# Seven quarter products in place of eight for the latent keys and six gate tiles

## The chip, the cores and the metric

The kernel runs on one core of a Trainium2 chip. Its time is the device time of one execution in microseconds (us); three runs gave 587.22 to 587.62, median 587.51. A core has five engines with a queue of instructions each, worked off in order: TensorE (PE) multiplies matrices into PSUM, VectorE (DVE) and ScalarE (ACT) do elementwise work on SBUF and PSUM, GpSimd (POOL) on SBUF alone, and SyncE (SP) issues most DMA transfers. They wait for each other through semaphores.

## The reference

The input is x, 1024 positions by 1024 channels, in float32. One layer of multi-head latent attention with eight heads is computed, then a last RMS norm:

```python
h = rms_norm(x, l0_norm)
proj = h @ w_in          # c_q 384 | c_kv 256 | k_pe 64 | gate 1024
q  = rms_norm(c_q, q_norm) @ w_uq       # per head 128 + 64 rotary
kv = rms_norm(c_kv, kv_norm) @ w_ukv    # per head k 128, v 128
q_pe, k_pe = apply_rope(q_pe), apply_rope(k_pe)
p = softmax((q_nope @ k_nope.T + q_pe @ k_pe.T) * 192 ** -0.5)
o = p @ v
y = x + (o * silu(gate)) @ w_out
return rms_norm(y, final_norm)
```

## The kernel before

**Three matmuls for one product.** Each float32 operand is split into a high part (rounded to the type that PE takes) and a low part, the rest. A product of two operands is then three matmuls: high x high, high x low, low x high. This is `mm3` (L58 to L61). A split is one copy for the high part and one subtraction on DVE for the low part; for weights `split` (L63) makes the copy on POOL.

**Stages.** First x, transposed, comes in as eight blocks of 128 channels (L161 to L187). Each is scaled with the norm's gain, split into `xh` and `xl`, and multiplied at once with the weights of the query latents, which gather in six PSUM banks. Then come ten tiles of 128 output columns over the same x (`stream`, L252): two of latent keys, one for the rotary part of the key (with half the matmuls for each block), and eight gate tiles (`stream_gate`, L268). A tile is 8 blocks of channels x 2 halves of the positions x 3 = 48 matmuls of 128x128 by 128x512 into one PSUM pair of banks (`wide`, two of them). Its weights come in two loads of 256 KB; two raw buffers (`gwr`) and three split ones (`gwh`, `gwl`) serve all tiles.

Between them DVE, ACT and POOL compute three norms. The norm of x is not applied to x but to each product, as a row `rx_sb`. Its sums of squares come from a second load of x, in natural order (`rstd_x`, L213). The latents' sums of squares (`latent_sums`, `total`) go over PE and through DRAM (`spread`, `latent_norm`), and come back as rows broadcast over all partitions; `latent_scale` (L247) applies them. Then `rope_half` (L344) makes the rotary part of the queries in four halves of 18 matmuls: DVE and POOL rotate, ACT and DVE split, and SP writes the parts to DRAM (`qpe_d`), from where attention loads them by head. These halves stand between gate tiles 1 to 4; gate tiles 5 to 7 follow them.

After that come the attention with softmax over 64 blocks of queries, and the output product.

**What sets the order.** A planner at build time orders each engine's instructions by a simulation of the program, with the order in the source as priority. `later` and `tc.issue_after` bend this. Within an engine's queue the order is then fixed.

The few lines that matter most:

```python
wr = gp.tile([P, 4, P], F32, name=f"gwr_{m}_{kq}", tag="gwr", bufs=2)
nc.sync.dma_start(wr, wg[m - 3 - (m > 5), :, kq * 4:(kq + 1) * 4])
split(wr, wh[-1], wl[-1])
...
for i in range(1, H):
    stream_gate(i)
    ...
    if i < 5:
        g, half = (i - 1) // 2, (i - 1) % 2
        rope_half(g, half, w_rope[g])
```

Of the kernel before, what the change touches and what calls it, by code (L numbers as in the profile page):

```python
# [14 lines left out]
P = 128  # L15
L = 1024
# [13 lines left out]
def kernel(  # L30
# [20 lines left out]

    nc = tc.nc
# [5 lines left out]
    def mm3(ps, lh, ll, rh, rl, first, last):  # L58
        mm(ps, lhsT=lh, rhs=rh, start=first, stop=False)  # L59
        mm(ps, lhsT=lh, rhs=rl, start=False, stop=False)  # L60
        mm(ps, lhsT=ll, rhs=rh, start=False, stop=last)  # L61
# [57 lines left out]
    rw = xctx.enter_context(tc.tile_pool(name="rw", bufs=2, side="right"))  # L119
# [4 lines left out]
    def total(ssq, half, name):  # L124
# [6 lines left out]
        nc.gpsimd.tensor_add(top, top, src[0:DR])  # L131
# [13 lines left out]

    with ExitStack() as wctx:
        wp = wctx.enter_context(tc.tile_pool(name="wp", bufs=3))
# [13 lines left out]
        for k in range(KD):  # L161
# [14 lines left out]
            for hs in [halves(0), halves(1)] if k < 3 else [slice(0, L)]:  # L176
# [4 lines left out]
                )  # L181
            units = [(m, half) for half in range(2) for m in range(3)]
# [11 lines left out]
    gpool = ctx.enter_context(tc.tile_pool(name="gate", bufs=1))  # L194
    gate = gpool.tile([P, H, L], F32, name="gate")
    cctx = ExitStack()
    wts = cctx.enter_context(tc.tile_pool(name="wts", bufs=1))
    kvp = cctx.enter_context(tc.tile_pool(name="kvp", bufs=1))
    kv_h = kvp.tile([P, 2, L], F32R, name="kv_h")
    kv_l = kvp.tile([P, 2, L], F32R, name="kv_l")  # L200
# [12 lines left out]
    def rstd_x():  # L213

        rows = x.rearrange("(p j) c -> p j c", j=KD)
        for j in range(KD):
            xn = home[1][:, 1 + j % 3]
            nc.sync.dma_start(xn, rows[:, j])
            nc.scalar.activation(xn, xn, AF.Square, accum_out=ssx[:, j:j + 1])
        nc.vector.tensor_scalar(v_s, ssx, 1.0 / D, EPS, op0=ALU.mult, op1=ALU.add)  # L220
# [4 lines left out]
    def latent_sums(ms, name):  # L225
        cs, sq = gate[:, 4], gate[:, 5]
        for i, m in enumerate(ms):
            if i == 0:
                nc.scalar.activation(cs, craw[m], AF.Square)
            else:  # L230
                nc.scalar.activation(sq, craw[m], AF.Square)
                nc.gpsimd.tensor_add(cs, cs, sq)
        line = gate[0:1, 6]
# [18 lines left out]
    def stream(m):  # L252
        wh, wl = [], []
        for kq in range(2):
            wh.append(gp.tile([P, 4, P], F32R, name=f"gwh_{m}_{kq}", tag="gwh"))
            wl.append(gp.tile([P, 4, P], F32R, name=f"gwl_{m}_{kq}", tag="gwl"))
            wr = gp.tile([P, 4, P], F32, name=f"gwr_{m}_{kq}", tag="gwr", bufs=2)
            nc.sync.dma_start(wr, wg[m - 3 - (m > 5), :, kq * 4:(kq + 1) * 4])
            split(wr, wh[-1], wl[-1])
        ps = wide(f"g_{m}")  # L260
        for k in range(KD):
            for half in range(2):
                hs = halves(half)
                mm3(ps[:, hs], wh[k // 4][:, k % 4], wl[k // 4][:, k % 4], xh[:, k, hs], xl[:, k, hs],
                    k == 0, k == KD - 1)
        return ps

    def stream_gate(i):  # L268
        ps = stream(6 + i)
        gt = gate[:, i]  # L270
        nc.vector.tensor_mul(gt, ps, rx_sb)
        nc.scalar.activation(gt, gt, AF.Silu)

    rstd_x()
    ps = stream(3)
    nc.scalar.copy(craw[3], ps)
    latent_sums((0, 1, 2), "sq")
    ps = stream(4)
    nc.scalar.copy(craw[4], ps)
    latent_norm("sq", QR, "rq", gate[:, 7])  # L280
    latent_sums((3, 4), "sk")

    wr = gp.tile([P, KD, DR], F32, name="wpe_r", tag="gwr", bufs=2)
# [11 lines left out]
    rk_sb = gate[0:DR, 1:3]  # L297
    nc.sync.dma_start(rk_sb, rope_k)
    kp = home[1][:, 3]
    nc.vector.tensor_mul(kp, ps, rx_sb)  # L300
# [12 lines left out]
    latent_scale((0, 1, 2), gate[:, 7])  # L313
    latent_norm("sk", KR, "rk", gate[:, 7])
    cqp = cctx.enter_context(tc.tile_pool(name="cqp", bufs=1))
# [5 lines left out]
    stream_gate(0)  # L321
# [9 lines left out]
    def load_q(src, pool=None):  # L331
# [474 lines left out]
```

## Time and profile before

| | |
|---|---|
| median of three runs | 587.51 us |
| the profiled execution | 587.4 us |
| its span, first to last instruction | 585.7 us |
| PE busy | 571.8 us (98%), 2604 matmuls |
| DVE busy | 425.4 us (73%) |
| ACT busy | 275.5 us (47%) |
| POOL busy | 233.8 us (40%) |
| mean granted TensorE clock | 0.993 |

Times in views of the trace count from the start of the span. A row of a timeline gives start, duration, engine, source line, operation and the tiles it writes and reads; idle time before it stands in brackets with what ended it. A row of a group gives the line, the shapes and the count, then busy time in us and mean ns of one, then idle time before. A row by stretches gives the busy time of each engine, the granted clock as a share of full speed, the DMA engines' busy share and GB/s. "L65" is line 65 of the kernel. A busy PE need not be at its peak, since matmuls overlap; their spacing says more than their duration.

### The profile page before, as it was taken

The page shows a single profiled execution, that of the slowest core. Times are in us where ns is not written, and L with a number is a line of the kernel's source. Part 1 is how long each engine was busy: PE and PEld are TensorE (multiplying, and loading weights), DVE is VectorE, ACT ScalarE, POOL GpSimd, SP SyncE. Part 2 cuts the span into 40 slices and gives each one's busy share as a digit, 9 for nine tenths or more (in the row PEclk, how much of TensorE's full clock was granted, in tenths as well). Part 3 has the DMA queues.
Part 4 walks back from the last instruction along what each step waited for, and adds up shares of the span by engine and source line. Part 5 has one row for each costly group of instructions (what it writes and reads, how often), then busy time and mean ns, then how long its engine had stood idle before and what let it go on. Part 6 is the DMA issues. An engine that isn't in the chain of part 4 may idle for free.

```text
span 585.7 us, 7657 instructions
## 1 busy us (share of the span) xinstructions
PE 571.8 (98%) x2604; PEld 472.8 (81%) x2604; DVE 425.4 (73%) x573; ACT 275.5 (47%) x438; POOL 233.8 (40%) x201
## 2 busy tenths in 40 slices
PE   9999999999999999999999999999999979999995
PEld 5888888888888878888888888888888858788885
DVE  4923589475236799988888988898888894984663
ACT  4348463021014455553655455645365662644652
POOL 1623512343102345643553535533434874683000
PEclk9999999999999999999999999999999979999999
DMA  8766221324211448674457464763476458521332
GB/s 263 275 206 245 95 74 38 124 93 141 109 38 46 94 117 193 154 171 109 107 132 179 105 153 109 168 148 94 100 162 147 132 135 213 198 77 54 138 132 107
DMA packets 35962, 78.66 MB, mean 134 GB/s; under 512 B 7314, under 2 KB 11154, under 8 KB 35860
## 3 DMA queue, kind: packets, MB, share of 16 engines
q1 hardware_dynamic: 34628, 76.21, 48.3%
q10 hardware_dynamic: 1296, 1.97, 0.9%
q8 instruction: 20, 0.33, 0.2%
q14 instruction: 18, 0.15, 0.1%
HBM read 36.19 MB, written 8.41 MB: 76 GB/s over the span
## 4 chain that ended last, share of the span: by engine, by line
PE 90%; SPq 3%; DVE 2%; ACT 1%; DMA 1%; issue 1%; POOL 0%; DVEq 0%; ACTq 0%; POOLq 0%
PE g L59 6%; PE g L61 6%; PE g L60 6%; PE o L59 5%; PE o L60 5%; PE o L61 5%; PE pv L60 5%; PE pv L59 5%; PE pv L61 5%; PE s L59 4%; PE s L60 4%; PE s L459 4%; PE s L61 4%; PE s L458 4%; SPq L481 3%; PE q L59 2%
## 5 line engine op out<-in xcount | busy, mean ns | idle before, releaser
L472 POOL TENSOR_SCALAR probs<-probs,rc 128x1024 f32<-128x1024 f32 x64 | 84.3, 1319 | 113.0 <-DVE rc L471 108.9
L466 ACT ACTIVATE probs<-s,nmx 128x1024 f32<-128x1024 f32 x64 | 71.6, 1118 | 113.3 <-DVE nmx L464 110.4
L473 DVE STREAM_TRANSPOSE probs<-probs 128x1024 f32<-128x1024 f32 x64 | 79.2, 1238 | 15.8 <-POOL probs L472 14.2
L464 DVE TENSOR_REDUCE nmx<-s 128x1 f32<-128x1024 f32 x64 | 76.0, 1207 | 3.8 <-PE s L459 3.7
L488 ACT CAST pt_h<-d 128x1024 fp32r<-128x1024 f32 x64 | 65.3, 1052 | 8.0 <-PE pv L61 4.9
L59 PE MATMUL g<-xh,gwh 128*128 128x512 f32 x160 | 62.2, 389 | 0.0
L60 PE MATMUL g<-xl,gwh 128*128 128x512 f32 x160 | 62.2, 389 | 0.0
L61 PE MATMUL g<-xh,gwl 128*128 128x512 f32 x160 | 62.2, 389 | 0.0
L493 POOL TENSOR_TENSOR pt_l<-d,pt_h 128x512 fp32r<-128x512 f32 x32 | 49.1, 1534 | 26.0 <-ACT pt_h L488 25.3
L60 PE MATMUL pv<-pt_l,v_h 128*128 128x512 f32 x128 | 50.3, 393 | 2.4 <-POOL pt_l L493 2.0
L59 PE MATMUL s<-k_h,q_h 128*128 128x512 f32 x128 | 50.2, 392 | 1.2 <-ACT probs L466 1.2
L490 DVE TENSOR_TENSOR pt_l<-d,pt_h 128x1024 fp32r<-128x1024 f32 x32 | 48.8, 1524 | 3.5 <-ACT pt_h L488 3.3
L59 PE MATMUL pv<-pt_h,v_h 128*128 128x512 f32 x128 | 50.1, 392 | 0.0
L60 PE MATMUL s<-k_l,q_h 128*128 128x512 f32 x128 | 49.9, 390 | 0.0
L61 PE MATMUL pv<-pt_h,v_l 128*128 128x512 f32 x128 | 49.9, 389 | 0.0
L61 PE MATMUL s<-k_h,q_l 128*128 128x512 f32 x128 | 49.9, 389 | 0.0
L458 PE MATMUL s<-kk_h,qpe 128*128 128x512 f32 x128 | 49.8, 389 | 0.0
L459 PE MATMUL s<-kk_l,qpe 128*128 128x512 f32 x128 | 49.8, 389 | 0.0
L59 PE MATMUL o<-woh,o_split 128*128 128x512 f32 (+1 forms) x118 | 45.8, 388 | 2.5 <-ACT o_split L575 2.5
L60 PE MATMUL o<-wol,o_split 128*128 128x512 f32 (+1 forms) x118 | 45.6, 386 | 0.0
L61 PE MATMUL o<-woh,o_split 128*128 128x512 f32 (+1 forms) x118 | 44.5, 383 | 0.0
L576 DVE TENSOR_TENSOR o_split<-gate,o_split 128x512 fp32r<-128x512 f32 (+2 forms) x48 | 32.5, 708 | 9.4 <-ACT o_split L575 9.3
(194 smaller groups left out, 1237.1 us busy)
## 6 DMA issues: line engine op xcount, KB each, us to landing
d<-probs SPq DMA_DIRECT2D x256, 128.0 KB
gwr<-in_wg SPq DMA_DIRECT2D x20, 256.0 KB
craw_b<-in_x SPq DMA_DIRECT2D x8, 512.0 KB
qpe<-qpe_d SPq DMA_DIRECT2D x16, 256.0 KB
wor<-in_wo SPq DMA_DIRECT2D x16, 256.0 KB
xr<-in_x SPq DMA_DIRECT2D x16, 256.0 KB
xr<-in_xT SPq DMA_DIRECT2D x5, 512.0 KB
qpe_d<-craw_a SPq DMA_DIRECT2D x8, 256.0 KB
```

The lines of the kernel that those rows point to most:

```text
L59: mm(ps, lhsT=lh, rhs=rh, start=first, stop=False)
L60: mm(ps, lhsT=lh, rhs=rl, start=False, stop=False)
L61: mm(ps, lhsT=ll, rhs=rh, start=False, stop=last)
L458: mm(s[:, ks], lhsT=qpe_s, rhs=kk_h[:, ks], start=False, stop=False)
L459: mm(s[:, ks], lhsT=qpe_s, rhs=kk_l[:, ks], start=False, stop=True)
L464: maxima[u] = nc.vector.tensor_reduce(nmx, s, axis=AX.X, op=ALU.max, negate=True)
L466: exps[u] = nc.scalar.activation(p_t.rearrange("p j k c -> p k j c"), s.rearrange("p (k j c) -> p k j c", k=8, j=4), AF.Exp, bias=nmx, acc ...
L472: nc.gpsimd.tensor_scalar(p_t, p_t, rc, 1.0, op0=ALU.mult, op1=ALU.mult)
L473: nc.vector.transpose(out=p_t, in_=p_t)
L488: nc.scalar.copy(hi, src)
L490: nc.vector.tensor_sub(lo, src, f32(hi))
L493: nc.gpsimd.tensor_sub(lo[:, 2:4], src[:, 2:4], f32(hi[:, 2:4]))
```

## The change

The latent keys' two tiles, and gate tiles 0/4, 1/5 and 2/6, are computed in pairs by a scheme with seven products in place of eight (Strassen's, in Winograd's form). With the two tiles of weights and x each cut in quarters (a tile x half of the channels; half of the channels x half of the positions), a pair is a 2 x 2 product of quarters. Sums of weight quarters (on DVE, for each pair) meet sums of quarters of x (t1 to t4, made once). The seven products land in separate PSUM banks, and DVE adds them into the four results.

- t1, the difference of x's halves, is made while x is loaded. `combine_x` makes t2, t3 and t4; t3 takes the place of the quarter `x12`, which `restore_x12` later loads and splits again.
- `split_act` makes the high part of weights on ACT in place of POOL; the sums of squares add on DVE in place of POOL.
- `g_load` has seven raw buffers; `gwh` and `gwl` keep three.
- Gate tiles 3 and 7 stay as they were, but in halves of 24 matmuls (`gate_half`), one before each of the four rotary halves, which now come last before attention.
- The key's rotary product comes first; its scaling by `rx_sb`, the norms and the scalings move between the pairs.
- Six gates get `rx_sb` and SiLU from SBUF in `gate_end`; the rotary weights are loaded after the pairs.

```diff
 def total(ssq, half, name):
-        nc.gpsimd.tensor_add(top, top, src[0:DR])
+        nc.vector.tensor_add(top, top, src[0:DR])
...
+    t1, = t_parts("t1")
+    t3 = x12
+    def split_gained(raw, k, hl):
+        hi, lo = (t[:, k % 4] for t in hl)
+        g = g_sb[:, k:k + 1]
+        nc.scalar.activation(hi, raw, AF.Copy, scale=g)
+        nc.vector.scalar_tensor_tensor(lo, raw, g, f32(hi), op0=ALU.mult, op1=ALU.subtract)
...
+            if k < 4:
+                nc.vector.tensor_sub(raw_a[:, k], xr[:, halves(1)], xr[:, halves(0)])
+                split_gained(raw_a[:, k], k, t1)
...
-                nc.gpsimd.tensor_add(cs, cs, sq)
+                nc.vector.tensor_add(cs, cs, sq)
...
+    def split_act(src, hl):
+        hi, lo = hl
+        nc.scalar.copy(hi, src)
+        return nc.vector.tensor_sub(lo, src, f32(hi))
+
+    def combine_x():
+        for k in range(4):
+            nc.vector.scalar_tensor_tensor(
+                raw_a[:, k], raw_a[:, k], g_sb[:, k:k + 1], f32(x22[0][:, k]), op0=ALU.mult, op1=ALU.subtract
+            )
+        nc.vector.tensor_sub(raw_a, raw_a, f32(x22[1]))
+        split_act(raw_a, t2)
+        nc.vector.tensor_add(raw_b, raw_a, f32(x11[0]))
+        nc.vector.tensor_add(raw_b, raw_b, f32(x11[1]))
+        split_act(raw_b, t3)
+        nc.vector.tensor_add(raw_a, raw_a, f32(x21[0]))
+        nc.vector.tensor_add(raw_a, raw_a, f32(x21[1]))
+        return split_act(raw_a, t4)
+
+    def g_load(w, j):
+        raw = gp.tile([P, 4, P], F32, name=f"gwr_{w}_{j}", tag="gwr", bufs=7)
+        nc.sync.dma_start(raw, wg[w, :, 4 * j:4 * j + 4])
+        return raw
+
+    def product(ps, w, x_part):
+        for k in range(4):
+            last = mm3(ps, w[0][:, k], w[1][:, k], x_part[0][:, k], x_part[1][:, k], k == 0, k == 3)
+        return last
+
+    def pair_start(a, b, dst_a, dst_b):
+        r11, r12 = g_load(a, 0), g_load(a, 1)
+        ps = wide("g")
+        p1, p2 = ps[:, 0:HT], ps[:, HT:L]
+        product(p1, g_parts(r11), x11)
+        nc.scalar.copy(dst_a[:, 0:HT], p1)
+        product(p2, g_parts(r12), x21)
+        return a, b, dst_a, dst_b, r11, r12, p2
+
+    def pair_end(state):
...
+        nc.vector.tensor_add(s, r21, r22)
+        p5 = acc("g")
+        product(p5, g_parts(s), t1)
+        nc.vector.tensor_sub(s, r11, s)
+        p6 = ps_t.tile([P, HT], F32, name="g", tag="t")
+        product(p6, g_parts(s), t2)
+        nc.vector.tensor_add(c12, p6, c11)
+        nc.vector.tensor_add(c11, p2, c11)
+        nc.vector.tensor_sub(r21, r21, r11)
+        p7 = acc("g")
+        middle = product(p7, g_parts(r21), t3)
+        nc.vector.tensor_add(c21, p7, c12)
+        nc.vector.tensor_add(c22, p5, c21)
+        nc.vector.tensor_add(c12, p5, c12)
+        nc.vector.tensor_add(s, r12, s)
+        p3 = ps_t.tile([P, HT], F32, name="g", tag="t")
+        product(p3, g_parts(s), x22)
+        nc.vector.tensor_add(c12, p3, c12)
+        p4 = acc("g")
+        product(p4, g_parts(r22), t4)
+        nc.vector.tensor_add(c21, p4, c21)
+        return middle
...
+    first = pair_start(0, 1, craw[3], craw[4])
+    pairs = [gate_start(0)]
+    with tc.issue_after(combine_x().ins):
+        norm_x()
+    pair_end(first)
+    pairs.append(gate_start(1))
+    middle = pair_end(pairs[0])
+    with tc.issue_after(middle.ins):
+        latent_sums((0, 1, 2), "sq")
+    gate_end(0)
+    pairs.append(gate_start(2))
...
+    latent_norm("sq", QR, "rq", home[1][:, 3])
+    middle = pair_end(pairs[1])
+    with tc.issue_after(middle.ins):
+        latent_sums((3, 4), "sk")
+    gate_end(1)
+    latent_scale((0, 1, 2), home[1][:, 3])
+    latent_norm("sk", KR, "rk", gate[:, 7])
+    pair_end(pairs[2])
+    gate_end(2)
+    latent_scale((3, 4), gate[:, 7])
...
-            ab.append(acc("ab"))
+            ab.append(acc("ab") if half == 0 else ps_t.tile([P, HT], F32, name="ab", tag="t"))
...
+    w_rope = [load_q(wqp[j]) for j in range(2)]
+    restore_x12()
+    gate_half(3, 0, direct)
...
+    rope_half(0, 0, w_rope)
+    gate_half(3, 1, direct)
+    rope_half(0, 1, w_rope)
+    w_rope = [load_q(wqp[2 + j]) for j in range(2)]
+    gate_half(7, 0, direct)
+    for m in range(2):
+        nc.scalar.copy(kv_h[:, m], craw[3 + m])
+        nc.vector.tensor_sub(kv_l[:, m], craw[3 + m], f32(kv_h[:, m]))
+    rope_half(1, 0, w_rope)
+    gate_half(7, 1, direct)
+    rope_half(1, 1, w_rope)
```

More of the change, by code (lines that the diff above doesn't have):

```diff
@@ L192 @@
         nc.vector.tensor_copy(craw[2][:, HT:L], a_5)
[L194 to L200, printed above, removed]
+    t2, t4 = t_parts("t2", "t4")
     rx_sb = xs.tile([P, L], F32, name="rx_sb")
@@ L225, in latent_sums @@
     def latent_sums(ms, name):
[L226 removed]
+        cs, sq = home[1][:, 1], home[1][:, 2]
         for i, m in enumerate(ms):
@@ L250, in latent_scale @@
             nc.vector.scalar_tensor_tensor(c, c, g_sb[:, KD + m:KD + m + 1], row, op0=ALU.mult, op1=ALU.mult)
[L252 to L260, printed above, removed]
-        for k in range(KD):
[L262 to L266, printed above, removed]
@@ new lines, in g_parts @@
+    def g_parts(src, shape=(P, 4, P)):
+        wh = gp.tile(list(shape), F32R, name="gwh", tag="gwh")
+        wl = gp.tile(list(shape), F32R, name="gwl", tag="gwl")
+        split_act(src, (wh, wl))
+        return wh, wl
+    def g_load(w, j):
[6 more added lines that the diff above has]
+        return last
@@ new lines, in gate_end, with gate_start, restore_x12 @@
+    def gate_end(i):
+        for j in (i, 4 + i):
+            nc.vector.tensor_mul(gate[:, j], gate[:, j], rx_sb)
+            nc.scalar.activation(gate[:, j], gate[:, j], AF.Silu)
+    def gate_start(i):
+        return pair_start(2 + i, 6 + i, gate[:, i], gate[:, 4 + i])
+    def restore_x12():
+        for k in range(4):
+            raw = gp.tile([P, HT], F32, name=f"xr2_{k}", tag="gwr", bufs=7)
+            nc.sync.dma_start(raw, xT[k * P:(k + 1) * P, halves(1)])
+            split_gained(raw, k, x12)
@@ new lines, in gate_half @@
+    def gate_half(i, half, state):
+        if half == 0:
+            state[i] = wide("g"), [g_parts(g_load(2 + i, j)) for j in range(2)]
+        ps, w = state[i]
+        hs = halves(half)
+        for k in range(KD):
+            mm3(ps[:, hs], w[k // 4][0][:, k % 4], w[k // 4][1][:, k % 4], xh[:, k, hs], xl[:, k, hs],
+                k == 0, k == KD - 1)
+        if half:
+            nc.vector.tensor_mul(gate[:, i], ps, rx_sb)
+            nc.scalar.activation(gate[:, i], gate[:, i], AF.Silu)
@@ L286 @@
+    squares_x()
+    wr = gp.tile([P, KD, DR], F32, name="wpe_r", tag="gwr", bufs=7)
     nc.sync.dma_start(wr, wpe)
```

72 lines of the change are left out of this document (32 added, 40 removed).

## The prediction

> **What bounds the kernel now.** I read the head of the page first, then busy time by stage, then what TensorE (PE) waits for.
>
> ```profile
> span 585.7 us, 7657 instructions
> PE 571.8 (98%) x2604; PEld 472.8 (81%) x2604; DVE 425.4 (73%) x573; ACT 275.5 (47%) x438; POOL 233.8 (40%) x201
> ```
> ```profile
> core 0: us, PE busy (x) PEld busy (x) DVE busy (x) ACT busy (x) POOL busy (x), PEclk, DMA share, GB/s
> 0.00:37.70 37.70, 36.33 (x152) 27.81 (x152) 23.44 (x30) 12.82 (x15) 13.07 (x20) 1.00 0.76 254
> 37.70:171.60 133.90, 133.90 (x592) 110.70 (x591) 70.19 (x95) 49.30 (x66) 41.56 (x37) 1.00 0.33 110
> 171.60:182.00 10.40, 10.40 (x53) 8.86 (x52) 6.05 (x9) 3.81 (x6) 1.54 (x3) 1.00 0.26 83
> 212.00:450.00 238.00, 238.00 (x1119) 199.75 (x1118) 211.07 (x262) 124.91 (x187) 111.65 (x89) 1.00 0.59 135
> ```
> ```profile
> PE o L59 <- ACT o_split L575: 2.5, 1, 2.5
> PE pv L60 <- POOL pt_l L493: 2.0, 2, 1.1
> PE s L59 <- ACT probs L466: 1.2, 2, 0.9
> ```
>
> The stretch 37.70 to 171.60 is the one the diff rewrites: latent keys, eight gate tiles, rotary products. PE is busy for all of its 133.90 us, and the longest waits PE has anywhere belong to the attention (pv, s) or the output product (o), not to the gate tile g. So this stage is as long as its 592 matmuls: 133.90 / 592 = 0.226 us each. VectorE (DVE) stands at 70.19 / 133.90 = 52% there, ScalarE (ACT) at 37%, GpSimd (POOL) at 31%. The profiled execution took 587.4 us (span 585.7 and 1.7 around it); the median of the runs shown is 587.51, the same within 0.02%.
>
> **What goes: matmuls.** A pair of weight tiles took 2 x 8 x 2 x 3 = 96 matmuls; seven quarter products of 4 x 3 take 84. Four pairs (keys, and gates 0/4, 1/5, 2/6) save 48, each still 512 columns wide with its own weight load, so 48 x 0.226 = **-10.9 us** if PE stays as dense. Gates 3 and 7 keep their 96; the key's rotary part keeps 32, the rotary products 72, the sums 4.
>
> **What comes: DVE work.** These rows carry the prices and what is taken away:
>
> ```profile
> L65 DVE TENSOR_TENSOR gwl<-gwr,gwh 128x512 fp32r<-128x512 f32 x17 | 12.5, 733 | 22.2 <-POOL gwh L64 22.1
> L271 DVE TENSOR_TENSOR gate<-g,rx_sb 128x1024 f32<-128x1024 f32 x8 | 9.7, 1215 | 7.8 <-PE g L61 7.8
> L357 DVE TENSOR_TENSOR craw_a<-ab,craw_b 128x512 f32<-128x512 f32 x8 | 5.1, 678 | 0.0
> L320 DVE TENSOR_TENSOR cq_l<-craw_a,cq_h 128x1024 fp32r<-128x1024 f32 x3 | 3.5, 1207 | 0.0
> L375 DVE TENSOR_TENSOR kv_l<-craw_a,kv_h 128x1024 fp32r<-128x1024 f32 x1 | 2.1, 2053 | 1.0 <-POOL kv_h L374 1.0
> L143 DVE TENSOR_TENSOR small<-small 128x8 f32<-128x8 f32 x3 | 2.6, 881 | 0.1
> L241 DVE TENSOR_TENSOR small<-small 128x8 f32<-128x8 f32 x2 | 0.3, 164 | 1.3 <-DMA small<-sq_d 1.3
> ```
> ```profile
> 37.92 0.39 PE L59 MATMUL g<-xh,gwh 128*128 128x512 f32 x1
> 29.07 1.27 DVE L178 SCALAR_TENSOR_TENSOR xl<-xr,g_sb,xh 128x1024 fp32r<-128x1024 f32 x1
> 85.39 3.48 DVE L320 TENSOR_TENSOR cq_l<-craw_a,cq_h 128x1024 fp32r<-128x1024 f32 x3
> 94.09 1.28 DVE L357 TENSOR_TENSOR craw_a<-ab,craw_b 128x512 f32<-128x512 f32 x2
> ```
>
> Two 512-element operations back to back take 1.28 us, so 0.64 each, PSUM operand or not (L357 reads PSUM). Three of 1024 take 3.48, so 1.16. An operation over 2048 is not in the trace: twice the 1024 one is 2.3, the lower end 2.2 (1207 ns and two more steps of 1207 - 691), the upper 2.4 (two separate ones); I take 2.3.
>
> Added on DVE:
> - Pairs: each has 7 low-part subtractions, 4 weight sums, 7 sums with a PSUM operand: 18 x 4 x 0.64 = 46.1.
> - combine_x: 4 of 512, and 8 of 2048 (five sums or differences, three low parts): 2.6 + 18.4 = 21.0.
> - The six gates' scaling by rx_sb (gate_end) 6 x 1.16 = 7.0; gates 3 and 7, 4 x 0.64 + 2 x 1.16 = 4.9; the restored quarter of x, 4 x 0.64 = 2.6.
> - Taken over from POOL in the sums of squares (L232, L131): 3 x 1.16 + 4 x 0.64 = 6.0.
>
> That is 87.6. Of the 70.19 now spent, 12.5 (L65) and 9.7 (L271) go, leaving 48.0. Some of that was slowed while POOL ran beside it (2053 ns against 1207 for the same shape in L375, 881 against 164 for 8 elements in L143); I take 4 off. The splits of rotary weights, done under the loads now, move in with 2.2. Total 87.6 + 44.0 + 2.2 = 133.8 us. Outside the stage fall about 6 us of combine_x, since DVE has its last low part of x at 29.07 + 1.27 = 30.3 and PE starts the first gate product only at 37.92; four early weight splits, 2.6; and the last rotary half, 6 x 0.64 = 3.8. So **121.4 us of DVE in a stage of 133.9 - 10.9 = 123.0: 99%.** DVE becomes as full as PE.
>
> ```profile
> 80.00:100.00 20.00, 20.00 (x90) 16.57 (x89) 19.11 (x24) 11.53 (x13) 4.45 (x5) 1.00 0.13 40
> ```
>
> The densest stretch of this stage now has DVE at 19.11 of 20 us (96%) with PE not waiting; in the long attention stretch it is 211.07 of 238.00 (89%), again with a full PE. At 96% the work lasts 121.4 / 0.956 = 127.0, or **+4.0 us** of PE waits; at 100% none; at 89% it lasts 136.9, or +13.9. A gain is excluded: PE has no wait here to lose. I take 96%, the row of this very stage, and keep both ends.
>
> Where would the waits sit? Weight parts have three buffers. Each held 24 matmuls and now holds 12, so two buffers ahead cover 2 x 12 x 0.226 = 5.4 us instead of 10.9. PE needs gate weights at once after the first pairs, while DVE in the stretch between the third and fourth pair also has the key's rotation, both norms, five latent scalings, the query splits. There the two totals meet.
>
> **ACT, POOL and the loads.** ACT takes the high parts: 32 copies of 512 for pairs, 3 of 2048, four of 512 each for gates 3/7 and restored x.
>
> ```profile
> L191 ACT COPY craw_a<-acc 128x512 f32<-128x512 f32 x1 | 0.6, 587 | 1.0 <-PE acc L61 1.0
> L319 ACT CAST cq_h<-craw_a 128x1024 fp32r<-128x1024 f32 x3 | 3.2, 1056 | 5.3 <-DVE craw_a L250 5.0
> L64 POOL TENSOR_SCALAR gwh<-gwr 128x512 fp32r<-128x512 f32 x20 | 15.9, 796 | 44.2 <-DMA gwr<-in_wg 24.2 <-PE g L60 19.4 <-PE pe L296 0.4
> ```
>
> At 0.59 and 1.06 (2.1 for 2048) that is 19 + 6 + 5 = 30 us on top of 49.30: 65% of 123, off the path while DVE is fuller. POOL loses its 20 splits (15.9 us), which hides nothing and costs nothing. Under the loads, the difference of x's halves for k < 4 adds 8 DVE operations of 512, 5.1 us, and four on ACT. DVE there is busy 23.44 of 37.70 and sheds the three gate and five other weight splits, so I take **+0.4**, ends 0 and 5.1. The load buffer xr is held one subtraction (0.64) longer, and SP issues the next x behind it; from k = 4 on that is slack. SP's weight loads are the same tiles, seven buffers instead of two; four more loads of 256 KB bring x's quarter back.
>
> **Entry to attention.** Gates 5 to 7 stood between the last rotary half and attention; now the rotary products come last.
>
> ```profile
> 123.89 2.13 SPq L363 DMA_DIRECT2D qpe_d<-craw_b  x2
> 136.86 0.69 DVE L361 TENSOR_TENSOR craw_b<-craw_a,craw_b 128x512 fp32r<-128x512 f32 x1 [4.87 <-DMA qpe_d<-craw_b]
> 171.56 1.23 DVE L271 TENSOR_TENSOR gate<-g,rx_sb 128x1024 f32<-128x1024 f32 x1 [7.80 <-PE g L61]
> ```
> ```profile
> DVE craw_b L361 <- DMA qpe_d<-craw_b: 6.7, 2, 4.9
> ACT craw_b L360 <- DMA qpe_d<-craw_b: 2.7, 1, 2.7
> DVE craw_a L250 <- DMA gate<-rk_d: 7.3, 1, 7.3
> ```
>
> The writes of a rotary half to DRAM are issued from 123.89, and the buffer they read was free only at 136.86; DVE waited 4.9 us for it, ACT 2.7. Now that is harmless: gate work follows until 171.56. After the change the halves come every 24 + 18 matmuls (9.5 us), less than the 13 us a buffer stays taken, and behind the blocked subtraction stand the splits of the first k, q and v, for which the first scores wait. Bounds: -1.2, if the scores' one wait (s, above) goes too; 7.6 = 4.9 + 2.7, if both waits come in full. I take **+1.0**, between, nearer the small end: heads 4 to 7 alone need the last half, and DVE is busy only 6.05 of the 10.40 us from 171.60.
>
> The same kind of wait inside the stage: the scaling L250 stood 7.3 us on a broadcast row, with a gate's splits queued behind it. Before, 10.9 us of buffered products covered that; 5.4 leave 1.9 open. This is in the 96%.
>
> **Sum:** 587.4 - 10.9 + 4.0 + 0.4 + 1.0 = **581.9 us**.
>
> [...] How long is a gap before the clock drops?
>
> ```profile
> 476.00:478.00 2.00, 1.14 (x3) 0.70 (x4) 2.00 (x5) 2.00 (x4) 0.88 (x1) 0.50 0.45 166
> 478.00:480.00 2.00, 2.00 (x6) 1.62 (x6) 2.00 (x3) 2.00 (x3) 2.00 (x2) 0.50 0.00 0
> 476.86 0.80 PE L59 MATMUL o<-woh,o_split 128*128 128x512 f32 x1 [2.46 <-ACT o_split L575]
> 480.96 0.63 PE L59 MATMUL o<-woh,o_split 128*128 128x512 f32 x1
> 481.38 0.63 PE L60 MATMUL o<-wol,o_split 128*128 128x512 f32 x1
> 482.10 0.40 PE L59 MATMUL o<-woh,o_split 128*128 128x512 f32 x1
> 482.33 0.39 PE L60 MATMUL o<-wol,o_split 128*128 128x512 f32 x1
> ```
>
> After a gap of 2.46 us (with two shorter ones before it) the granted clock is 0.50 and matmuls start 0.42 us apart until about 482, then 0.23: some 5 us at half speed, 2.4 lost. Were my 4.0 us one gap, they would cost 6.4. [...]
>
> **Rivals.**
> 1. Everything fits: the planner's order keeps DVE ahead, small terms vanish: 587.4 - 10.9 = **576.5**. For it: 121.4 is below 123.0, and PE can take the direct gates' matmuls in a gap. Against: no stretch here shows DVE at 99%.
> 2. Other side: DVE becomes the bound, from the point where it gets less than 121.4 / 133.9 = 91% of its time used, since then the stage is no shorter than today. In-order DVE waits for ACT's copy in each of 28 splits, for PE in each of 28 PSUM sums, and for broadcast rows. At attention's 89%: 587.4 - 10.9 + 13.9 + 1.4 = **591.8**. For it: dependent sums follow each other in each pair. Against: a planner orders other ready work between.
> 3. The rotary writes stall the entry in full: 581.9 - 1.0 + 7.6 = **588.5**, no change. For it: 9.5 against 13 us. Against: the writes then share the queue with fewer weight loads.
> That the matmuls do not go is excluded by the count.
>
> **Chances.** Forecast (579 to 585) 0.45; rival 1 0.26; rival 2 0.15; rival 3 0.14. About 0.2% (1.2 us) is what a measurement tells from no change. Faster holds the first two and a little of the third (0.03): 0.74. Same: most of the third, 0.09. Slower: the second and the rest, 0.17. The range goes from just under rival 1 to just over rival 3, **575.8 to 589.0**, and leaves out rival 2's far end.
>
> **What would show it.** Right: 432 instead of 480 matmuls of g; PE at 0.226 apart inside a product; DVE above 93% from 37 to 160; PE waits naming DVE low parts (gwl) between the second and fourth pair, each under 1 us, 3 to 5 in sum; the last rotary matmul near 165. Rival 1: no PE wait before the first scores. Rival 2: waits on gwl or on PSUM sums in every pair, over 10 us, with DVE itself idle on ACT or DMA. Rival 3: PE idle over 5 us before the first scores, with L361's successor waiting for qpe_d writes. I am wrong altogether if the loads (first 37 us) grow by over 2 us, or PE's clock falls in this stage.

## The result, and the profile after

The changed kernel takes **618.63 us** (median of 4 runs, 616.52 to 622.38), the kernel before 587.57 beside it (4 runs, 587.22 to 587.64): a ratio of **1.0537, 95% interval 1.0484 to 1.059**. It was made for fewer matmuls and is 31 us slower; the forecast was 581.9, with 589.0 as the upper end. The profiled execution of the changed kernel took 622.38 us, 34.8 us more span than the profiled one of before. That is 3.8 us over the median, so sums from its profile come out that much higher. One of the four executions of the kernel of run 8, the profiled one, fell into a slower state (637.76 us at a granted clock of 0.85) and is left out of that run's numbers.

The head of the page of the changed kernel:

```profile
span 620.5 us, 7702 instructions
PE 572.7 (92%) x2556; PEld 468.7 (76%) x2556; DVE 480.4 (77%) x660; ACT 308.6 (50%) x488; POOL 202.4 (33%) x172
```

2556 matmuls against 2604: the 48 are gone. But PE is busy 92% of the span, not 98%. Busy time by stage (columns: the stretch in us, its length, busy time and instructions of PE, weight load, DVE, ACT, POOL, the granted clock, DMA share, GB/s), first after, then the two stretches of before that answer to the last two:

```profile
37.70:178.50 140.80, 129.60 (x541) 102.91 (x539) 110.55 (x156) 77.08 (x107) 10.46 (x8) 0.96 0.29 90
178.50:210.30 31.80, 12.16 (x43) 9.88 (x43) 12.07 (x19) 5.59 (x9) 6.53 (x7) 0.68 0.36 122
210.30:620.50 410.20, 394.45 (x1824) 327.56 (x1822) 324.56 (x445) 209.93 (x353) 178.10 (x143) 0.99 0.53 132
```
```profile
171.60:179.62 8.02, 8.02 (x42) 6.88 (x41) 5.02 (x7) 3.21 (x5) 1.13 (x2) 1.00 0.31 96
179.62:585.70 406.08, 393.55 (x1823) 327.38 (x1821) 326.70 (x443) 210.19 (x353) 178.08 (x142) 0.99 0.53 132
```

The stages part at the last rotary matmul (178.50; before, the last gate matmul, 171.60) and at the first score matmul (210.30; 179.62). So the 34.8 us split like this (the first stage of before is the prediction's row from 37.70 to 171.60):

| stage | before | after | difference |
|---|---|---|---|
| gates, keys, rotary products | 133.90 | 140.80 | +6.9 (10.9 fewer matmuls, 17.8 lost) |
| to the first scores | 8.02 | 31.80 | +23.8 |
| from the first scores to the end | 406.08 | 410.20 | +4.1 |

Of the 17.8 us lost in the first stage, PE stood idle for 11.2 (140.80 less 129.60). The other 6.6 went while it was busy, at a granted clock of 0.96 against 1.00 before.

Waits of PE in the changed kernel (total, times, longest), and DVE's for the writes of the rotary halves:

```profile
PE k L62 <- DVE craw_a L475: 17.0, 1, 17.0
PE sum_sk L137 <- DVE ss_b L135: 4.0, 1, 4.0
PE v L62 <- POOL wv_h L67: 2.6, 1, 2.6
PE g L62 <- ACT gwh L278: 2.6, 3, 1.4
PE k L62 <- POOL wk_h L67: 2.0, 1, 2.0
PE g L64 <- DVE gwl L279: 1.5, 2, 0.8
PE g L62 <- ACT gate L317: 1.5, 2, 1.3
PE g L62 <- ACT craw_a L317: 1.3, 1, 1.3
```
```profile
DVE craw_a L478 <- DMA qpe_d<-craw_a: 12.3, 3, 5.4
DVE craw_b L478 <- DMA qpe_d<-craw_b: 6.1, 1, 6.1
```

One wait of 17.0 us makes half of the loss: the first key product waits for DVE's last rotary sums (L475 reads the PSUM bank that it needs), and those stand in DVE's queue behind subtractions (L478) that wait for buffers which the writes to DRAM still read. Two rows of that queue show it; the key product starts at 195.4:

```profile
191.84 0.69 DVE L478 TENSOR_TENSOR craw_b<-craw_a,craw_b 128x512 fp32r<-128x512 f32 x1 [6.11 <-DMA qpe_d<-craw_b]
194.11 1.28 DVE L475 TENSOR_TENSOR craw_a<-ab,craw_b 128x512 f32<-128x512 f32 x2
```

**Two bounds inside the first stage.** The same columns for shorter stretches of the changed kernel:

```profile
40.00:60.00 20.00, 15.22 (x63) 11.32 (x62) 15.70 (x14) 19.66 (x29) 0.00 (x0) 0.99 0.38 130
120.00:140.00 20.00, 16.04 (x61) 12.73 (x60) 17.00 (x26) 10.52 (x15) 0.00 (x0) 0.83 0.25 82
```
```profile
59.60:63.40 3.80, 3.80 (x11) 2.94 (x11) 2.21 (x6) 1.15 (x2) 0.00 (x0) 0.55 0.21 70
```

From 40 to 60 it is ACT that has no room, 19.66 of 20, while POOL does nothing. PE waits four times for 0.8 to 1.4 us, and then its clock is near one half from 59.6 to 63.4 (11 matmuls in 3.8 us). From 120 to 140 PE waits 4 us for the latent sums. DVE's queue shows why (start, duration, idle before):

```profile
121.03 3.68 DVE L274 SCALAR_TENSOR_TENSOR craw_a<-craw_a,g_sb,craw_b 128x1024 f32<-128x1024 f32 x3 [2.44 <-DMA craw_b<-rq_d]
124.62 1.22 DVE L351 TENSOR_TENSOR gate<-gate,rx_sb 128x1024 f32<-128x1024 f32 x1
125.87 0.69 DVE L135 TENSOR_TENSOR ss_b<-ss_t,ss_b 64x512 fp32r<-64x512 f32 x1
```
```profile
126.61 0.79 PE L137 MATMUL sum_sk<-ss_b,ones 128*128 128x512 f32 x1 [3.96 <-DVE ss_b L135]
127.20 0.63 PE L62 MATMUL g<-t_h,gwh 128*128 128x512 f32 x1
127.63 0.63 PE L63 MATMUL g<-t_l,gwh 128*128 128x512 f32 x1
```

DVE stood 2.44 us on a row that comes back from DRAM, then did three scalings and a gate, and only then the short subtraction that PE needed. PE then goes on with a matmul every 0.43 us, at a granted clock of 0.50 from 126.6 to 131.0.

**Why the writes last.** SP's issues of the writes, before and after (count, ns of an issue, first and last start), then, for the changed kernel from 184 to 204 in steps of 0.5 us, the busy share of the 16 DMA engines in tenths and the rate of all transfers:

```profile
L363 SPq DMA_DIRECT2D qpe_d<-craw_a x8: 509/521/619, 100.8 to 146.6; - x8
L363 SPq DMA_DIRECT2D qpe_d<-craw_b x8: 503/701/1329, 102.8 to 149.1; - x8
```
```profile
L480 SPq DMA_DIRECT2D qpe_d<-craw_a x8: 508/520/632, 163.8 to 201.5; - x8
L480 SPq DMA_DIRECT2D qpe_d<-craw_b x8: 503/517/533, 165.2 to 206.5; - x8
```
```profile
DMA  2222686222222232222222247996222222222222
GB/s 86 80 84 81 132 299 238 107 98 102 98 86 98 98 94 57 57 41 90 82 98 111 98 119 147 373 418 242 98 98 111 102 98 94 107 98 102 90 107 98
```

While writes pass, the rate is a steady 98 GB/s or so, with the engines busy two tenths of the time; only with the loads and reads among them (issued at 184.47, 193.62 and 195.34) does it go to 240 to 420. At 100 GB/s one write of 256 KB takes 2.6 us, the four of a half 10.5, and all 16 take 42 us: 163.8 + 42 = 206, and the last one is issued at 206.5. Before, the same 16 writes lay between 101 and 149 under gate products. The first weights of attention are issued on the same queue among the writes.

### The profile page after: what moved, and what is told of

Same layout as the page of the kernel before. It is cut to its first block, busy times and chain, and to the rows that moved or that the text cites. A ratio compares the mean times of both kernels' runs of the same rounds, so it can differ in the third digit from the quotient of the medians.

```text
span 620.5 us, 7702 instructions
## 1 busy us (share of the span) xinstructions
PE 572.7 (92%) x2556; PEld 468.7 (76%) x2556; DVE 480.4 (77%) x660; ACT 308.6 (50%) x488; POOL 202.4 (33%) x172
## 4 chain that ended last, share of the span: by engine, by line
PE 42%; DVE 6%; POOL 4%; issue 4%; ACT 4%; SPq 2%; DMA 1%; DVEq 0%; ACTq 0%; POOLq 0%
PE o L62 5%; PE o L63 5%; PE o L64 5%; PE pv L62 3%; PE pv L63 3%; POOL probs L593 3%; PE pv L64 3%; PE s L62 2%; PE s L64 2%; PE s L63 2%; PE s L579 2%; PE s L580 2%; ACT probs L587 2%; DVE nmx L585 2%; SPq L602 2%
## 5 line engine op out<-in xcount | busy, mean ns | idle before, releaser
L67 POOL TENSOR_SCALAR wq_h<-wq_r 128x384 fp32r<-128x384 f32 x12 | 10.1, 845 | 153.0 <-DMA wq_r<-in_wqp 121.6
L62 PE MATMUL g<-xh,gwh 128*128 128x512 f32 x96 | 38.5, 401 | 3.9 <-ACT gate L317 1.5
L63 PE MATMUL g<-xl,gwh 128*128 128x512 f32 x96 | 38.0, 396 | 0.0
L64 PE MATMUL g<-xh,gwl 128*128 128x512 f32 x96 | 37.9, 397 | 0.0
```

The costliest lines, as they stand in the source:

```text
L64: return mm(ps, lhsT=ll, rhs=rh, start=False, stop=last)
```

## The experiments

All ratios are against the kernel before, run on the same chip in the same session (587.5 to 587.9 us there). "The changed kernel" is 618.63, from a session of its own; its four executions spread over 5.9 us, so a difference to it of 2 or 3 us says little.

**1. Another buffer for the odd halves.** The high and low parts of every second half go to two of the weight loads' buffers.

```diff
             hi, lo = hl[:, 0:HT], hl[:, HT:L]
+            if half:
+                hi, lo = (gp.tile([P, HT], F32, name=f"room_{c}", tag="gwr", bufs=7) for c in "hl")
```

> Changed kernel with one edit: the odd rotary halves put their split parts in free weight buffers, so a half no longer has to wait until the writes of the half before it have left their buffer. Theory W (DVE and ACT stand in their queues on buffers that the writes of the rotary parts still read; the first k, q, v and the PSUM banks wait behind them): the wait of the first k, 17.0 us in the changed kernel, falls below 5 us, and the time falls by 12 to 22 us, to 597 to 607. Rival P (the chain of DVE, GpSimd and ACT of the last rotary half is long by itself, and k waits for the PSUM bank whatever the writes do): the wait stays above 10 us and the time falls by less than 5 us.

Measured: 626.84 us, ratio 1.0655 [1.0619, 1.0691], 8 us slower than the changed kernel, so both expected times missed. The wait of 17 us is gone, and others stand in its place:

```profile
PE g L62 <- ACT gwh L278: 14.1, 3, 13.0
PE v L62 <- POOL wv_h L67: 7.3, 1, 7.3
```

The weight loads of gate 7 share their buffers with the writes now, and its products wait 13.0 us for a split. The wait moved with the buffer; freeing the buffer did not free the time.

**2. The same PSUM banks for all halves.**

```diff
-            ab.append(acc("ab") if half == 0 else ps_t.tile([P, HT], F32, name="ab", tag="t"))
+            ab.append(acc("ab"))
```

> Changed kernel with one edit: the odd rotary halves take the same two PSUM banks as the even ones, as in the kernel before, so that two other banks are free for the first k. Theory W (writes hold the buffers): PE waits in front of the last rotary half instead of in front of k, for about the same time; total within 4 us of the changed kernel (614 to 623). Rival P (only the choice of the bank makes k wait): the 17 us wait goes and the time falls by 10 us or more.

Measured: 641.81 us, 1.0921 [1.0905, 1.0937]; both expectations missed. The first key product still waits 10.6 us, and rotary and key products wait another 8.9 and 5.3. The choice of banks in the change is not the cause; undoing it costs 23 us more.

**3. The latent sums one pair later.** `latent_sums((3, 4), "sk")` and what depends on it move from the third pair into the fourth.

```diff
-    middle = pair_end(pairs[1])
-    with tc.issue_after(middle.ins):
-        latent_sums((3, 4), "sk")
+    pair_end(pairs[1])
...
+    middle = pair_end(pairs[2])
+    with tc.issue_after(middle.ins):
+        latent_sums((3, 4), "sk")
```

> Changed kernel with one edit: the sum of squares of the key latents stands inside the fourth pair instead of the third. Theory Q (its PE matmul waits 4.0 us for a DVE subtraction that is queued behind scalings which wait for a broadcast row, and the clock halves afterwards, some 2 us more): 3 to 7 us faster than the changed kernel. Rival D (DVE is simply full, and the wait turns up at another place): within 2 us of it. The rotary end of the stage is as before, so the first k still waits over 10 us in both.

Measured: 620.78 us, 1.0568 [1.0536, 1.0599], no gain: theory Q missed, and rival D's 2 us are passed by 0.15. The wait for the sums is gone, and its time comes back:

```profile
PE k L62 <- DVE craw_a L475: 14.2, 1, 14.2
PE s L64 <- DVE q_l L552: 7.6, 1, 7.6
PE g L64 <- DVE gwl L279: 5.0, 3, 3.7
```

**4. High parts of the weights on GpSimd again.**

```diff
-        split_act(src, (wh, wl))
+        split(src, wh, wl)
         return wh, wl
```

> Changed kernel with one edit: GpSimd makes the high parts of the gate and key weights again, as in the kernel before, instead of ACT. Theory A (from 40 to 60 us ACT is the bound: busy 19.66 of 20 us, and weights' high parts queue behind squares of x and the casts of combined x): the PE waits before 64 us, about 5 us with 2 us of half clock after them, shrink below 2 us and the time falls by 4 to 8 us. Rival D (DVE is the bound, and runs slower beside GpSimd): no gain, or up to 6 us slower.

Measured: 614.98 us, 1.0465 [1.0449, 1.048], 3.7 us better: rival D falls, and theory A's 4 to 8 us are just missed. The slowest of its executions, 616.13, lies just under the changed kernel's quickest, 616.52. In its profile PE's waits before 64 us shrink to one of 1.7 and the last rotary matmul comes 6 us earlier, but the key product still waits 15.7 us. So ACT's load in the first 20 us is a real cost, and the entry eats a part of what is won.

**5. Spare buffers that nobody else wants.** By the time of the second rotary group the key latents are split and their buffers free. The group's first half uses them.

```diff
+            if (g, half) == (1, 0):
+                hl = spare[i]          # craw[3], craw[4]
             hi, lo = hl[:, 0:HT], hl[:, HT:L]
```

> Edit: the first half of the second rotary group puts its high and low parts into the two buffers of the key latents, which are free by then; nothing else moves, and no load shares a buffer with it. Theory W (the entry stalls because the last rotary halves wait for the writes of the half before): the wait of 17.0 us of the first k product for the rotary sums falls below 8 us and no VectorE wait on the qpe_d writes over 2 us stands after the first rotary group; 606 to 612 us. Rival Q (the wait moves on, to the loads of the first weights that stand on SP's queue behind the writes): the first score product starts within 3 us of the changed kernel's; 616 to 621 us.

Measured: 619.79 us, 1.0538 [1.0497, 1.0579], no change in the median.

```profile
PE k L62 <- DVE craw_a L478: 11.5, 1, 11.5
PE v L62 <- POOL wv_h L67: 4.4, 1, 4.4
```

The key product waits 5.5 us less, the value product 1.8 more, and the median stays. Theory W, in which the buffers were the cause, falls with this run: both its wait (under 8 us) and its 606 to 612 missed. Rival Q had the time right but not its sign: in the profile the first scores start at 204.35, 6 us before the changed kernel's, not within 3. The two profiled executions lie 6.1 us apart themselves (616.27 against 622.38), so that sign settles little, and its reason, that the loads behind the writes come late, was not tested.

**6. Both at once.**

> Edit: the spare buffers as in the run before it, and the high parts of the gate weights on GpSimd instead of ScalarE. If the two losses are separate and add: 3.65 us less than the spare buffers alone give (602 to 609 us under theory W, 612 to 617 under rival Q). If whatever is saved early is waited for again at the entry: no more than 1 us less than the better of the two edits alone.

The diffs of runs 4 and 5 together. Measured: 615.43 us, 1.047 [1.0454, 1.0487], as good as the high parts on GpSimd alone. They don't add, as the second expectation had it.

**7. The second half of gate 7 after the last rotary half**, with the spare buffers.

```diff
-    gate_half(7, 0, direct)
     for m in range(2):
...
     rope_half(1, 0, w_rope)
-    gate_half(7, 1, direct)
+    gate_half(7, 0, direct)
     rope_half(1, 1, w_rope)
+    gate_half(7, 1, direct)
```

> Edit: the spare buffers again, and the order of the last work changed: all but the last rotary half stand before gate 7, whose second half (24 matmuls, 5.4 us) comes after the last rotary half. Theory C (the entry stalls because no products are left behind the last rotary half): TensorE idles at the entry at least 4 us less than with the spare buffers alone, 600 to 607 us. Rival Q: the gate's own weights or the first keys' weights come late, and the time stays within 2 us of the spare buffers alone, or rises.

Measured: 628.24 us, 1.0694 [1.0671, 1.0716]: worse. The key product waits 14.7 us, and the next one 9.0 us for its weights. Theory C falls: 24 products put behind the last half did not cover the wait, and the weights behind the writes came later still.

**8. Two pairs instead of four.** Only the latent keys and gates 0/4 go by seven products, with the high parts on GpSimd; gates 1 and 2 by eight quarters ahead of the query parts, then 5, 6, 3 and 7 with the rotary halves between. The rotary halves take the same PSUM banks again, as in run 2. It saves 24 matmuls.

```diff
-    pairs.append(gate_start(1))
...
-    pairs.append(gate_start(2))
+    restore_x12()
+    direct = {}
+    gate_half(1, 0, direct)
+    gate_half(1, 1, direct)
...
+    for n, i in enumerate((5, 6, 3, 7)):
+        gate_half(i, 0, direct)
+        if n < 2:
+            rope_half(0, n, w_rope)
...
+        if n == 2:
+            rope_half(1, 0, w_rope)
+        gate_half(i, 1, direct)
+        if n == 2:
+            rope_half(1, 1, w_rope)
```

> Edit: only two pairs by seven products (latent keys, gates 0 and 4), the high parts of all gate weights on GpSimd; the other six gates by eight quarters as before, gates 1 and 2 ahead of the query parts, 5, 6, 3 and 7 after them with the rotary halves between and gate 7's second half last. 24 matmuls fewer than before the change: -5.4 us if TensorE stays as dense. Theory W with C (stall only where rotary halves stand last and DVE is full): no wait over 5 us at the entry, 583 to 590 us. Rival D (each pair costs more in waits of its own than its 12 matmuls save): 594 to 605 us even with the gates last.

Measured: 601.20 us (median of three), 1.0223 [1.0201, 1.0245]. Theory W with C falls, and the time lies in rival D's range: 17.4 of the 31 us are gone, and it is still 13.4 us slower than before with 24 matmuls fewer. Whether the two pairs themselves cost this, as rival D says, is left to runs 11 and 15: part of it is the writes.

**9. The writes themselves.** So far every edit had moved the wait, and none had made the writes shorter. One write covers four heads' rows; in DRAM these were four separate runs of 32 rows. With part, head, row as the order they are one run of 128 rows, and a read of one head is four runs instead.

```diff
-    qpe_d = dram.tile([H, 4, 32, L], F32, name="qpe_d")
+    qpe_d = dram.tile([4, H * 32, L], F32, name="qpe_d")
...
-                nc.sync.dma_start(qpe_d[g * 4:(g + 1) * 4, c, :, hs], src)
+                nc.sync.dma_start(qpe_d[c, g * P:(g + 1) * P, hs], src)
```

> Edit: only the order of the rows in the DRAM tensor qpe_d changes, from head, part, row to part, head, row, so that a write of four heads' rows is one run of 128 rows and a read of one head is four runs of 32. Theory B (the entry is as long as the rotary writes: 16 writes of 256 KB at some 100 GB/s, 2.6 us each, 42 us in all from 163.8, with the first weights behind them on the one queue): the writes pass at over 200 GB/s, the wait of 17.0 us of the first k product falls below 6 us, 600 to 607 us. Rival I (the entry is a chain of engines in order, GpSimd, ScalarE and VectorE handing on, with the writes only one link): the wait stays over 10 us and the time within 613 to 621 us.

Measured: **604.19 us**, 1.0278 [1.0245, 1.0312]: 14.4 us better, from the order of rows alone, as theory B expected. PE's longest wait, and the rates from 165 to 190 in steps of 0.62 us:

```profile
PE k L62 <- DVE craw_a L475: 5.0, 1, 5.0
```
```profile
GB/s 10 0 0 341 82 380 205 41 0 23 367 102 380 374 141 287 293 26 0 23 374 46 318 357 328 144 115 187 233 92 383 138 98 190 390 354 98 102 98 105
```

17.0 has become 5.0. While the writes pass, the rate peaks at 340 to 390 GB/s with pauses between, and at the end the 98 to 105 GB/s is back: now the reads, two of them issued in this stretch, have four runs each.

**10. The same with the diffs of runs 4 and 5.**

> Edit: the order of rows in qpe_d, the spare buffers, and the high parts of the gate weights on GpSimd. Under theory B the entry and the early part are separate once the writes are quick, and what the high parts on GpSimd save early (3.65 us alone) is kept: 595 to 602 us, at least 3 us under the order of rows alone. Rival I: 609 to 616 us.

Measured: 598.56 us, 1.0185 [1.0168, 1.0202], 5.6 us under the run before: once the writes are quick, what is saved early is kept.

**11. The diff of run 9 in the kernel with two pairs.**

> Edit: the kernel with two pairs by seven products, with the order of rows in qpe_d. That kernel has the rotary halves between gates, with 48 products after the last one. If its remaining loss against before lies in the writes or what stands behind them on the queue: at least 4 us below its 601.4 us. If it lies in the two pairs themselves (VectorE and the clock in the first 80 us): 599 to 602 us.

Measured: 594.19 us, 1.0112 [1.0096, 1.0129], 7.0 us better. The slow writes cost there too, with 48 products behind the last half.

**12. The diff of run 9 in the kernel before: the price of the reads.**

> Edit: the kernel before the change, with the order of rows in qpe_d alone. It prices the other side of that edit, the reads of one head as four runs of 32 rows, where the writes are under gate work already: theory B says the reads become as slow as the writes were (about 2.6 us each), which attention hides but for the first head: 586.5 to 590 us. If slow reads are waited for on every head: 592 us or more.

Measured: 593.69 us, 1.0095 [1.0075, 1.0114]: 5.9 us slower. By the time this is the second expectation, but not by its reason. The order of rows helps the writes (340 to 390 GB/s at the peaks of run 9) and hurts the reads (98 to 105 at the end of its row); the new wait in that profile is the first score's for the query, whose weights stand behind a read:

```profile
PE s L61 <- DVE q_l L431: 2.6, 1, 2.6
```

The granted clock is 0.91 from 180 to 200, and by 200 us the profile is 27 matmuls behind that of before, some 6 us at 0.226 each. So the loss lies at the first head, and not at every one.

**13. Quick writes and quick reads.** The partitions are turned instead: the rotary products give row, then head (by the order of the weights' columns and of the table's rows), so a write has 32 runs of 4, and the reads stay as they were.

```diff
-                nc.sync.dma_start(qpe_d[g * 4:(g + 1) * 4, c, :, hs], src)
+                nc.sync.dma_start(qpe_d[g * 4:(g + 1) * 4, c, :, hs].rearrange("h p t -> p h t"), src)
...
-        "wqp": uq[..., DN:].reshape(3, P, 2, 4, 2, 32).transpose(2, 4, 1, 0, 3, 5).reshape(4, P, 3, P),
+        "wqp": uq[..., DN:].reshape(3, P, 2, 4, 2, 32).transpose(2, 4, 1, 0, 5, 3).reshape(4, P, 3, P),
```

> Edit: instead of the order of rows in qpe_d, the order of the rotary outputs' partitions is turned (row of 32, then head, by the order of the weights' columns and of the table's rows), so that a write goes out as 32 runs of 4 heads while the reads stay as in the changed kernel. Theory B with the price of the slow reads from the kernel before (593.7 - 587.75 = 5.9 us): the writes pass at over 200 GB/s and the reads cost nothing, 604.2 - 5.9 = 598.3, so 596 to 601 us, and the writes and their queue own some 20 of the 31 us. If the rate does not follow the count of runs: 616 to 621 us.

Measured: **601.21 us**, 1.0221 [1.0192, 1.0249], just above the 596 to 601 expected: the slow writes cost the changed kernel **17.4 us** of its 31, somewhat fewer than the 20 expected. By the intervals of the two ratios the 17.4 is good to some 3.5 us. In the profile the stretch from the last rotary matmul to the first scores falls from 31.8 us to 14.7. The key product waits 4.9 us now, the sums 5.6. The rates from 165 to 185, in steps of 0.5 us:

```profile
GB/s 0 120 278 344 176 328 197 0 0 0 135 369 21 348 287 150 2 0 0 283 242 168 381 389 212 281 409 127 0 0 0 102 381 234 221 299 373 397 336 291
```

**14. Its control: the same edit in the kernel before.**

> Edit: the kernel before the change, with the turned partitions. Theory B: its writes lie under gate products, so quicker ones buy nothing: 587.2 to 588.3 us, no change. If quick writes shorten its entry too: under 586.5 us.

Measured: 587.54 us, 1.0003 [0.9994, 1.0011]. Before, the same slow writes cost nothing, since gate products covered them.

**15. Turned partitions with two pairs.**

> Edit: the kernel with two pairs, with the turned partitions (quick writes, quick reads). Theory B: 594.2 - 5.9 = 588.3, so 586.5 to 590 us. What then remains over 587.75 - 5.4 = 582.3 us is the waits of the two pairs themselves, before 90 us.

Measured: 589.77 us, **1.004 [1.0027, 1.0054]**, the nearest that any version came. No wait stands at the entry. PE's waits in the stage:

```profile
PE g L64 <- DVE gwl L68: 1.7, 1, 1.7
PE g L62 <- DVE gate L337: 0.9, 1, 0.9
PE g L62 <- DVE craw_b L337: 0.7, 1, 0.7
```

**16. A direct gate first**, so that its products cover the combinations of x (its scaling follows later). They are 48 matmuls, 10.9 us, half of the 21.7 us that the expectation gives.

```diff
+    gate_half(1, 0, direct)
+    gate_half(1, 1, direct, False)
     first = pair_start(0, 1, craw[3], craw[4])
...
-    gate_half(1, 0, direct)
-    gate_half(1, 1, direct)
+    gate_done(1)
```

> Edit: the run before it, with gate 1 by eight quarters ahead of the first pair (21.7 us of products that need none of the combined quarters), so that VectorE's combinations of x lie beside it. If the pairs' early waits come from VectorE and ScalarE being full just where the combinations are made: TensorE's waits from 38 to 90 us, 4 to 6 us with two pairs, fall to under 2 us, 584 to 587 us. If they come from each pair's own chain of splits and sums: within 1 us of the run before it.

Measured: 594.63 us, 1.0126 [1.0111, 1.0142], 4.9 us worse. The first wait is gone and a longer one of 2.2 us ends at 90.9, with a granted clock of 0.91 from 80 to 100. Both expectations missed.

**17. The first keys' products ahead of the key's rotary products**, in the kernel of run 15.

```diff
+    first = pair_start(0, 1, craw[3], craw[4])
     wr = gp.tile([P, KD, DR], F32, name="wpe_r", tag="gwr", bufs=7)
...
     nc.scalar.copy(kp, ps)
-    first = pair_start(0, 1, craw[3], craw[4])
```

> Edit: the kernel with two pairs and turned partitions, with the first two products of the latent keys (24 matmuls) ahead of the key's rotary products instead of behind them. In the profile of that kernel GpSimd splits the first keys' weights only when the rotary products free their buffers (42.3 and 46.0 us), and TensorE waits 1.71 us at 49 and then runs at half clock to 54.5, some 3.5 us in all. If that order makes the wait: it goes, 585.5 to 587.5 us. If VectorE's long combinations make it wherever the splits stand: 589 to 591 us.

Measured: 595.19 us, 1.0122 [1.0102, 1.0142], 5.4 us worse; both expectations missed. PE's longest wait for a gate's weights, and POOL's queue:

```profile
PE g L62 <- POOL gwh L67: 3.5, 2, 2.7
```
```profile
50.88 1.10 POOL L67 TENSOR_SCALAR gwh<-gwr 128x512 fp32r<-128x512 f32 x1 [2.72 <-PE g L63]
52.08 2.52 POOL L67 TENSOR_SCALAR gwh<-gws 128x512 fp32r<-128x512 f32 x1
59.60 0.64 POOL L67 TENSOR_SCALAR gwh<-gws 128x512 fp32r<-128x512 f32 x1 [5.00 <-PE g L63]
```

This order did not take the wait away. A copy that takes POOL 0.64 us takes 2.52 at 52 us; an operation of DVE over 2048 elements stands at 51.43 to 54.13 there.

**18. And the key's rotation later.**

```diff
+    latent_norm("sq", QR, "rq", home[1][:, 3])
+    gate_half(2, 0, direct)
     rk_sb = home[1][0:DR, 1:3]
...
-    latent_norm("sq", QR, "rq", home[1][:, 3])
-    gate_half(2, 0, direct)
```

> Edit: the run before it, and the rotation of the key (seven VectorE operations of 0.7 to 1.6 us) moved from the pair of gates 0 and 4 behind the first half of gate 2, where VectorE has room (13.2 of 20 us busy from 100 to 120). If VectorE's order there makes the waits of 0.7 and 0.9 us at 71 and 88: 1 to 2 us under the run before it. If not, the same within 0.7 us.

Measured: 595.53 us, 1.0134 [1.0118, 1.0149], the same as the run before it, as the second expectation had it.

## Why the prediction was wrong

Two terms of the sum failed: the entry to attention, taken as +1.0 and measured as 23.8 us with 4.1 behind it, and DVE's waits, taken as +4.0 and measured as 17.8. In the order of the sum:

**What goes (-10.9 us): right.** 2556 matmuls against 2604, at 0.23 us each where nothing waits.

**Loads (+0.4): nearly right.** The first product after the loads starts at 37.67, before at 37.92, so nothing was lost there.

**Durations: right.** The operation over 2048 elements, which no row of before had, was taken as 2.3 us:

```profile
L279 DVE TENSOR_TENSOR t_l<-gate,t_h 128x2048 fp32r<-128x2048 f32 x2 | 4.6, 2292 | 4.6 <-ACT t_h L278 4.6
```

**DVE at 96% (+4.0): wrong, 17.8 us.** The work was taken as 121.4 us and came to 110.55, but the step that failed is the one from a full engine to PE's waits. DVE was busy 110.55 of 140.80 us, 79%: it was not too full, it stood still for others, and PE waited for it and for ACT. Only 1.5 us of PE's waits name the low parts of weights, where the prediction had put 3 to 5. Rival 2 had put the point at which the gain is gone at 91%, and that point was passed. Three parts of the 17.8 show in the profile: the four waits before 60 us with a clock of 0.55 behind them, the wait of 4.0 us for the latent sums with 0.50 behind that, and several waits below 1 us. The 6.6 us at the lower clock (0.96 over the stage) are a part of the 17.8 for which the sum has no term. The prediction's remark that a scaling stands on a broadcast row with splits queued behind it named the second place, but put it "in the 96%"; in the run it was one gap of 4 us, and the granted clock behind it was 0.50.

**ACT at "65% of 123, off the path": wrong.** The total was right (77.08 us against 30 + 49.3 = 79). But the squares of x, the high parts of the combined x and those of the first weights all fall into the same 20 us, 19.66 of them busy. Taking the splits from POOL, of which the prediction said that it "hides nothing and costs nothing", leaves POOL at 0.00 there; giving them back saves 3.7 us alone and, together with spare buffers, 5.6 us once the entry is quick (runs 4 and 10). This is a mean over a stage used where one stretch decides.

**Entry to attention (+1.0, ends -1.2 and 7.6): wrong, 23.8 us and 4.1 behind it.** This is the step that failed most. The mechanism, halves every 9.5 us against a buffer that stays taken for 13, blocked subtractions and splits of k, q and v behind them, is what the profile shows, and it was rival 3, at a chance of 0.14. But its price was taken from the waits of before (4.9 + 2.7), which were so short because the 16 writes were spread over 48 us under gate products. The price to take was the transfer: 16 writes at about 100 GB/s are 42 us, while PE's products reach only 14.7 us beyond the first of them (163.8 to 178.5). The rate was there to read in the trace of before (128 to 148, steps of 0.5 us):

```profile
GB/s 127 332 332 361 152 98 106 98 107 98 107 86 90 78 78 131 98 102 98 111 98 102 98 111 98 270 250 180 242 295 156 188 250 266 102 98 111 98 98 102
```

The runs show it from both sides: more buffers (runs 1 and 5), other banks (run 2) and another order (run 7) only move the wait, quick writes remove 17.4 us (run 13), and before the change they are free (run 14). Of the 4.1 us behind the entry about 3 fall into the first 30 us of the scores: 132 matmuls there (210.3 to 240.3), before 145 (179.6 to 209.6).

Across the experiments the rate goes with how many separate runs a transfer has in DRAM: about 98 GB/s with 4 (the changed kernel), 340 to 390 at its peaks with 128 (run 9), up to 409 with 32 (run 13), and 98 to 105 again at the end of run 9's row, where the reads have 4. While it stays near 98, the DMA row of the changed kernel shows mostly the digit 2 (20 to 29% of the 16 engines); what holds it there is not shown.

**The clock.** The prediction read a granted clock of 0.50 behind a gap of 2.46 us, and its sum has no term for such a drop; its signs of being right had each wait for low parts under 1 us. The clock did fall in the stage, to 0.55 behind four waits of at most 1.43 us, which was one of the listed signs of being wrong altogether.

**What stays open.** With quick writes, 601.2 - 587.6 + 10.9 = 24.5 us are still lost. Its profiled run loses 19.1 in the stage (142.05 less 123.0) and 6.7 between the last rotary product and the first scores (14.7 against 8.02), where no gate stands behind the last half any more:

```profile
37.70:179.75 142.05, 130.62 (x544) 103.80 (x542) 115.82 (x163) 78.08 (x108) 11.03 (x11) 0.96 0.31 97
```

How much of the 19.1 each pair costs was not settled: two pairs lose 2.2 + 5.4 = 7.6 us against their own count (run 15), more than the 5.4 that they save, as rival D of run 8 had it, and each other order tried (runs 3, 16, 17, 18) moved waits to another place. That DVE's long operations slow POOL's copies fits run 17 (2.52 us for a copy beside one, 0.64 for another), but no run isolated it. No version tried is faster than the kernel before.

## What to carry to other kernels

Price a transfer that something waits for by its bytes and its own rate in the trace, not by the wait that it caused before: a wait hidden under other work says nothing of the transfer's length. When work moves to a place without cover, sum everything that must pass one queue from there on and set that against the compute beside it. And read how full an engine is over the stretch in which the new work lands, not over its stage.

## What the runs showed of the hardware

**A wait of 1.71 us was followed by a granted clock of 0.58 in one version and of 1.00 in another.** Two versions with two pairs (runs 11 and 15) wait 1.71 us at the same matmul, and then differ. The waiting matmul and the stretch behind it (columns as above, the granted clock third from the end), run 11, then run 15:

```profile
50.56 0.50 PE L64 MATMUL g<-xh,gwl 128*128 128x512 f32 x1 [1.71 <-DVE gwl L68]
```
```profile
50.40:54.70 4.30, 4.14 (x18) 3.45 (x19) 3.75 (x5) 3.68 (x6) 0.81 (x1) 1.00 0.05 15
```
```profile
50.84 0.50 PE L64 MATMUL g<-xh,gwl 128*128 128x512 f32 x1 [1.71 <-DVE gwl L68]
```
```profile
50.60:54.70 4.10, 3.86 (x10) 3.05 (x11) 2.98 (x3) 3.76 (x6) 0.00 (x0) 0.58 0.06 19
```

18 matmuls against 10 in about the same time, at a granted clock of 1.00 and 0.58. What makes the difference is not shown.

**The rate of the writes to DRAM changed with the count of their runs.** The same 256 KB pass at about 98 GB/s as four runs (the changed kernel), with peaks of 340 to 390 as 128 (run 9) and of up to 409 as 32 (run 13), by the rate of all transfers.

**GpSimd's copy of 128x512 elements varied fourfold**, from 0.64 to 2.52 us in one run (17), the two longest (2.50 us at 45.67, 2.52 at 52.08) while DVE is at work on operations over 2048 (from 45.40 and 51.43); that DVE is the cause is not shown.
